# Products' columns 112 bytes past the weights: x, sources, memory and weight buffers at new places

## The chip, the cores and the metric

One Trainium2 chip, one core. The metric is device time in microseconds of one execution of the program; a run's time is taken on the chip, and a profiled execution gives the trace.

## What is computed

Two layers of a streaming-encoder trunk on 256 tokens of width 1024, in float32. Each layer is half a SwiGLU FFN, a mixer, cross-attention to a memory of 256 tokens, and half an FFN again:

```python
for layer in range(DEPTH):                       # 2
    x = x + 0.5 * swiglu(rms_norm(x, ffn_norm[layer, 0]), ...)
    h = rms_norm(x, mix_norm[layer])
    if layer % 2 == 0:
        x = x + diff_stickbreak_mixer(h, ab_w_in[i], ab_w_out[i], ...)
    else:
        x = x + mla_mixer(h, mla_w_dq[i], ..., mla_w_o[i])
    x = x + memory_cross_attention(rms_norm(x, xm_norm[layer]), rms_norm(mem, xm_mem_norm[layer]), ...)
    x = x + 0.5 * swiglu(rms_norm(x, ffn_norm[layer, 1]), ...)

def swiglu(h, w_gate, w_up, w_down):             # 1024 -> 2816 -> 1024
    return (jax.nn.silu(h @ w_gate) * (h @ w_up)) @ w_down
```

All products with weights (gate, up, down, the projections of the mixers and of the cross-attention) read 190 MB of weights once.

## The kernel before

Each float32 operand of a weight product is split into a high and a low part in a 4-byte format that TensorE multiplies in one pass (F32R), and a product is the sum of three: high by high, high by low, low by high. In `mm3` (lines 290 to 292) these are three matmuls of 256 streamed columns. In `mm2` (lines 285 and 286), used for the down and output products, high and low of the source lie side by side and are streamed as one matmul of 512 columns over the high weights, and then the high part as one of 256 over the low weights. The first operand of a matmul is the side that is loaded into the array (128 columns), the second is the side that streams. The load for the next matmul (LDWEIGHTS) is an instruction of its own beside the running matmul.

Who is loaded and who streams: in `fm` and `fm_g` (gate and up of the FFNs, the query products and some of the mixers) the weights are loaded and x streams, 48 matmuls for one weight tile of 128 x 2048. In `tm_g` (the other projections of the first mixer, and keys and values of the memory) x or the memory is loaded and the weights stream, 48 matmuls also. In the two MLA products `kv_product` and `q_product` the latent sources are loaded. In `mm2` the weights are loaded and the sources stream.

Weights: `issue` starts the DMA of a weight tile (`wr`), ScalarE copies it into the high part (`wh`, line 247) and VectorE (for some pieces GpSimd) subtracts for the low part (`wl`, line 249). Three buffers of each (`HL = 3`) go round in turn. Each buffer is 64 columns wider than the weights, and `W_AT` says at which column they start in the buffer whose turn it is: 0, 16 or 32 (0, 64 or 128 bytes).

x: the two parts xh and xl stand in one tile each, 64 columns wider than the eight blocks of 256. `begin_phase` takes the next place of `X_AT` and `finish_dt` writes the scaled and split blocks of x there (lines 485, 486). The nine phases are: the input of the first FFN, then what the first mixer, the first cross-attention, the second and the third FFN, the second mixer, the second cross-attention and the last FFN read, and the output. The places before are 4, 4, 4, 12, 20, 20, 20, 28 and 0.

Sources: `Pair` takes a slot of 1024 columns (two blocks, high and low of each) from the arena. Each slot is a tile of 1032 columns, of which columns 4 to 1028 are used. The FFNs have 11 such slots, the mixers 6; the arena is opened anew for each of five stages. Memory: eight tiles of 512 columns, high and low of four pairs of blocks, written by `mem_gain` during an FFN.

The order of TensorE's instructions is the order in which the program is written (in the mixers a planner with given costs writes it); the other engines are ordered by the tile framework. Places in memory play no part in either.

Of the kernel before, what the change touches and what calls it, by code (L numbers as in the profile page):

```python
# [12 lines left out]
F32R = mybir.dt.float32r  # L13
# [6 lines left out]
P = 128  # L20
# [45 lines left out]
MLA_ORDER = (('k', 0), ('kv', 0), ('kv', 1), ('q', 0), ('q', 1), ('k', 1), ('q', 2), ('q', 3), ('v', 0))  # L66
HL = 3

W_AT = (0, 16, 32)
X_AT = (4, 4, 4, 12, 20, 20, 20, 28, 0)  # L70
SLOTS_MIX = (29, 12)

MEM_AT = (2, 4, 6, 8)
# [84 lines left out]
def trunk_kernel(ctx, tc, wflat, xT_d, xtok_d, memT_d, memtok_d, gains_d, rows_d, cst_d, out_d):  # L158
# [3 lines left out]
    wpool = ctx.enter_context(tc.tile_pool(name="w", bufs=1))  # L162
    cpool = ctx.enter_context(tc.tile_pool(name="c", bufs=1))
# [4 lines left out]
    def nm(s):  # L168
        uid[0] += 1
        return f"{s}_{uid[0]}"  # L170

    def T(tag, shape, bufs, dt=F32, pool=apool):
        return pool.tile(shape, dt, tag=tag, bufs=bufs, name=nm(tag))


    ar = {}

    @contextmanager
    def arena(n32, n32r):
        with tc.tile_pool(name=nm("ar"), bufs=1) as pool:  # L180
            ar["f"] = [pool.tile([P, 512], F32, name=nm("slotf")) for _ in range(n32)]
            ar["r"] = [pool.tile([P, 1032], F32R, name=nm("slotr"))[:, 4:1028] for _ in range(n32r // 2)]
            ar["own"] = {}
            yield
            assert not ar["own"]
# [26 lines left out]
    offs, o = [], 0  # L212
# [3 lines left out]
    loaded = {}  # L216
    issued = [0]

    turn = [0]

    def buffers(i):
        key, w = plan[i]
        small = w <= 256
        sfx, width = ("s", 256) if small else ("", 2048)
        raw = T("wr" + sfx, [P, width], 1 if small else RAW, F32, wpool)
        if small:
            return (raw, *(T(n + sfx, [P, width], 1, F32R, wpool) for n in ("wh", "wl")))
        o = W_AT[turn[0] % HL]
        turn[0] += 1
        lo = T("wl", [P, width + 64], HL, F32R, wpool)  # L230
        hi = T("wh", [P, width + 64], HL, F32R, wpool)
        return raw, hi[:, o:o + width], lo[:, o:o + width]

    def issue(i):
        raw, hi, lo = buffers(i)
        w = plan[i][1]
        name = plan[i][0][0] if isinstance(plan[i][0], tuple) else plan[i][0]
        step = SPLIT if name in ("gate", "up", "down") else SPLIT_MIX
        np_ = 0 if name in ("gate", "up", "down") else POOL_OF.get(name, 512)
        dstep = w if name in ("gate", "up", "down") else DSTEP  # L240
        src = wflat[offs[i]:offs[i] + P * w].rearrange("(p w) -> p w", p=P)
        for a in range(0, w, step):
            if a % dstep == 0:
                b = min(a + dstep, w)
                nc.sync.dma_start(raw[:, a:b], src[:, a:b])
            b = min(a + step, w)
            A.copy(hi[:, a:b], raw[:, a:b])  # L247
            e = G if a >= w - np_ else V
            e.tensor_tensor(out=lo[:, a:b], in0=raw[:, a:b], in1=hi[:, a:b].bitcast(F32), op=ALU.subtract)  # L249
        loaded[i] = (hi, lo)  # L250
# [4 lines left out]
    def issue_part(i, h, n):  # L255

        if h == 0:
            first[:] = buffers(i)
            loaded[i] = tuple(first[1:])
            issued[0] = i + 1  # L260
        raw, hi, lo = first
        w = plan[i][1]
        a0, a1 = h * (w // n), (h + 1) * (w // n)
        nc.sync.dma_start(raw[:, a0:a1], wflat[offs[i]:offs[i] + P * w].rearrange("(p w) -> p w", p=P)[:, a0:a1])
        return lambda: split_part(raw, hi, lo, a0, a1)
# [243 lines left out]
    parts = [cpool.tile([P, KT * S + 64], F32R, name="x" + h) for h in "hl"]  # L509
    x_at = list(X_AT)  # L510

# [277 lines left out]

    memstate = {}  # L790

    mem_hl = [cpool.tile([P, 512], F32R, name=f"mem{q}{h}") for q in range(4) for h in "hl"]
    memstate["rs"], msum = small[:, 16:18], small[:, 20:24]

    def mem_gain(l, q):
# [688 lines left out]
    with arena(*SLOTS_FFN):  # L1484
        begin_phase()
        for h in range(4):
            if h:
                nc.sync.dma_start(x[:, 2 * h:2 * h + 2, :], xT_d[:, 2 * h:2 * h + 2, :])
            split_w = issue_part(0, h, 4)
            if h == 0:  # L1490
                nc.sync.dma_start(gains[:, 0:NG], gains_d)
            for dt in (2 * h, 2 * h + 1):
                for made in finish_dt(dt, G_FFN):
                    pin(made)
            split_w()
        for h in range(2):
            issue_part(1, h, 2)()

        st.xg = st.nxt
        st.rs, st.var, st.rb = sl()[:, 0:2], sl()[:, 0:2], T("rb", [P, S], 1)  # L1500
        ss = sm()
        for q in range(4):
            xt = al()
            nc.sync.dma_start(xt, xtok_d[:, q // 2, (q % 2) * 512:(q % 2 + 1) * 512])
            A.activation(xt, xt, AF.Square, accum_out=ss[:, q:q + 1])
            rel(xt)
        nc.sync.dma_start(cst, cst_d[:, 0:512])
        V.tensor_reduce(out=st.var, in_=ss[:, 0:4].rearrange("p (a b) -> p a b", b=2), axis=AX.X, op=ALU.add)
        V.tensor_scalar(out=st.var, in0=st.var, scalar1=1.0 / D, scalar2=EPS, op0=ALU.mult, op1=ALU.add)
        rsqrt(st.var, 2, st.rs)  # L1510
        st.todo = [spread]
        ffn(0, 0, G_MIX, True, 0)
    with arena(*SLOTS_MIX):
        mixer_ab(G_XM)
        cross(0, G_FFN + 8)
    with arena(*SLOTS_FFN):
        ffn(0, 1, G_FFN + 16, True)
        ffn(1, 0, G_MIX + 8, False, 1)
# [80 lines left out]
```

## Time and profile before

| | us |
|---|---|
| median of 3 runs | 1115.44 (1114.12 to 1117.67) |
| profiled execution | 1115.93 |
| its span | 1114.2 |
| TensorE busy (matmuls) | 1091.3, 98% of the span |
| VectorE busy | 792.6, 71% |
| ScalarE busy | 654.6, 59% |
| mean granted clock of TensorE | 0.997 |

The span is from the first to the last instruction of the program in the trace; the profiled execution's own time has some 1.7 us around it. A busy share of TensorE says that it had a matmul in flight, not how fast matmuls follow one another; that is read from their starts.

### The profile page before, as it was taken

Reading aid. Unit: us, or ns where it says so; the run is one execution under the profiler, and the core shown is the slowest. Engines: PE = TensorE matmul, PEld = TensorE weight load, DVE = VectorE, ACT = ScalarE, POOL = GpSimd, SP = SyncE. Lnnn points to the kernel's source line nnn. Section 1 sums busy time; section 2 is a strip of 40 time slices with the busy share of each in tenths; the row PEclk is TensorE's granted clock in tenths of the full one; section 3 lists DMA queues with packets and bytes.
Section 4 is the critical chain, followed back from the end, with each engine's and each line's share of the span. In section 5 each row is a group of like instructions: output and inputs, shape, how many; then the busy total and the mean of one; then the engine's idle time right before and its main releaser. Section 6 shows DMA issues by size and latency. Waiting matters only on the chain.

```text
span 1114.2 us, 21671 instructions
## 1 busy us (share of the span) xinstructions
PE 1091.3 (98%) x8144; PEld 1032.4 (93%) x8144; DVE 792.6 (71%) x1930; ACT 654.6 (59%) x1775; POOL 198.7 (18%) x210
## 2 busy tenths in 40 slices
PE   8999999999899999999999999999989999999998
PEld 8999988998889899998899999889868899999987
DVE  6887766667866887775777776655688768877653
ACT  6676554667656665554555555555866556555542
POOL 2100001366334200000100000114871422000000
PEclk9999999999999999999999999999999999999999
DMA  8766556535335265555556554554341443655561
GB/s 294 242 238 211 180 181 204 190 97 170 114 114 189 88 215 190 189 180 183 186 184 222 179 210 173 190 189 161 105 131 60 152 149 119 225 189 190 182 222 51
DMA packets 50794, 193.25 MB, mean 173 GB/s; under 512 B 5760, under 2 KB 7552, under 8 KB 35584
## 3 DMA queue, kind: packets, MB, share of 16 engines
q1 hardware_dynamic: 50688, 191.86, 50.1%
q8 instruction: 64, 1.05, 0.4%
q14 instruction: 42, 0.34, 0.1%
HBM read 190.79 MB, written 1.05 MB: 172 GB/s over the span
## 4 chain that ended last, share of the span: by engine, by line
PE 85%; DVE 6%; ACT 3%; POOL 2%; issue 2%; DMA 2%; SPq 0%; DVEq 0%; POOLq 0%; ACTq 0%
PE mm L290 18%; PE mm L291 18%; PE mm L292 18%; PE mm L285 18%; PE mm L286 9%; DVE wl L249 2%; DMA wr<-wflat 2%; ACT slotf L766 1%; POOL sm L471 1%; PE t L779 1%; PE t L479 1%; PE s L1430 0%; PE s L903 0%; PE o L1463 0%; POOL sl L471 0%
## 5 line engine op out<-in xcount | busy, mean ns | idle before, releaser
L247 ACT CAST wh<-wr 128x256 fp32r<-128x256 f32 (+1 forms) x1216 | 440.8, 434 | 316.6 <-PE mm L291 155.4
L249 DVE TENSOR_TENSOR wl<-wr,wh 128x256 fp32r<-128x256 f32 (+1 forms) x1171 | 481.8, 465 | 125.1 <-ACT wh L247 117.7
L290 PE MATMUL mm<-xh,wh 128*128 128x256 f32 x1584 | 445.2, 281 | 2.7 <-ACT wh L269 1.7
L292 PE MATMUL mm<-xh,wl 128*128 128x256 f32 x1584 | 443.1, 280 | 0.1
L291 PE MATMUL mm<-xl,wh 128*128 128x256 f32 x1584 | 443.1, 280 | 0.0
L285 PE MATMUL mm<-slotr,wh 128*128 128x512 f32 x896 | 315.9, 396 | 1.1 <-DVE slotr L486 1.1
L290 PEld LDWEIGHTS mm<-xh,wh 128*128 128x128 f32 x1584 | 297.9, 188 | 4.1 <-ACT wh L269 2.1
L292 PEld LDWEIGHTS mm<-xh,wl 128*128 128x128 f32 x1584 | 298.2, 188 | 0.6 <-DVE wl L270 0.4
L291 PEld LDWEIGHTS mm<-xl,wh 128*128 128x128 f32 x1584 | 297.9, 188 | 0.3 <-DVE xl L486 0.2
L286 PE MATMUL mm<-slotr,wl 128*128 128x256 f32 x896 | 251.5, 281 | 0.0
L285 PEld LDWEIGHTS mm<-slotr,wh 128*128 128x128 f32 x896 | 168.5, 188 | 40.9 <-DVE slotr L486 1.4
L286 PEld LDWEIGHTS mm<-slotr,wl 128*128 128x128 f32 x896 | 168.8, 188 | 0.1
L543 POOL TENSOR_TENSOR acc<-acc,sq 128x256 f32<-128x256 f32 x49 | 43.3, 884 | 470.7 <-ACT sq L535 466.8
L249 POOL TENSOR_TENSOR wl<-wr,wh 128x512 fp32r<-128x512 f32 x45 | 66.8, 1485 | 108.6 <-ACT wh L247 108.6
L726 DVE TENSOR_TENSOR slotf<-mm,rb 128x512 f32<-128x512 f32 x44 | 30.3, 688 | 55.9 <-PE mm L292 55.9
L522 DVE SCALAR_TENSOR_TENSOR x<-mm,x 128x256 f32<-128x256 f32 x128 | 52.1, 416 | 21.3 <-PE mm L286 20.8
L485 ACT ACTIVATE xh<-x,gains 128x256 fp32r<-128x256 f32 x64 | 32.1, 507 | 33.2 <-DVE x L522 29.4
L718 DVE TENSOR_TENSOR slotf<-mm,rb 128x512 f32<-128x512 f32 x44 | 30.3, 688 | 26.0 <-PE mm L292 26.0
L766 ACT ACTIVATE slotf<-s,sm,sl 128x256 f32<-128x256 f32 (+1 forms) x64 | 32.8, 523 | 23.6 <-DVE sm L760 18.0
L486 DVE SCALAR_TENSOR_TENSOR xl<-x,gains,xh 128x256 fp32r<-128x256 f32 x64 | 39.1, 617 | 5.3 <-ACT xh L485 5.2
L491 DVE TENSOR_TENSOR slotr<-slotf,slotr 128x512 fp32r<-128x512 f32 (+1 forms) x52 | 35.5, 686 | 3.0 <-ACT slotr L490 2.6
L290 PE MATMUL mm<-wh,xh 128*128 128x256 f32 x128 | 37.2, 291 | 0.0
(218 smaller groups left out, 1086.1 us busy)
## 6 DMA issues: line engine op xcount, KB each, us to landing
wr<-wflat SPq DMA_DIRECT2D x118, 1024.0 KB, 4.8
wr<-wflat SPq DMA_DIRECT2D x180, 256.0 KB, 3.9
wr<-wflat SPq DMA_DIRECT2D x16, 768.0 KB, 4.4
slotf<-memT SPq DMA_DIRECT2D x8, 256.0 KB, 3.2
x<-xT SPq DMA_DIRECT2D x4, 256.0 KB, 4.7
wr<-wflat SPq DMA_DIRECT2D x2, 512.0 KB, 8.1
slotf<-xtok SPq DMA_DIRECT2D x4, 256.0 KB, 8.0
slotf<-memtok SPq DMA_DIRECT2D x4, 256.0 KB, 3.5
```

The source lines that it names most:

```text
L247: A.copy(hi[:, a:b], raw[:, a:b])
L249: e.tensor_tensor(out=lo[:, a:b], in0=raw[:, a:b], in1=hi[:, a:b].bitcast(F32), op=ALU.subtract)
L285: PE.matmul(bank[:, 0:512], w[0], src[2], start=first, stop=False)
L286: PE.matmul(bank[:, S:512], w[1], src[0], start=False, stop=last)
L290: PE.matmul(out, a[0], b[0], start=first, stop=False, **kw)
L291: PE.matmul(out, a[0], b[1], start=False, stop=False, **kw)
L292: PE.matmul(out, a[1], b[0], start=False, stop=last, **kw)
L486: V.scalar_tensor_tensor(out=lo, in0=src, scalar=g, in1=hi.bitcast(F32), op0=ALU.mult, op1=ALU.subtract))
L491: V.tensor_tensor(out=lo, in0=src, in1=hi.bitcast(F32), op=ALU.subtract)
L522: V.scalar_tensor_tensor(out=xd, in0=ps[:, h * S:(h + 1) * S], scalar=factor, in1=xd, op0=ALU.mult, op1=ALU.add)
L543: G.tensor_tensor(out=st.acc, in0=st.acc, in1=sq, op=ALU.add)
L766: A.activation(p[:, i * w:(i + 1) * w], sps[:, i * w:(i + 1) * w], AF.Exp, bias=nb[:, i:i + 1], scale=r, accum_out=sums[:, i:i + 1])
```

## The change

The weight buffers lose their extra columns and their turning places: all six start at the same residue by 256 bytes. The parts of x are written at column 28 (112 bytes) in all phases but the second, where it is column 36 (144 bytes). The source slots of an arena become pieces of one tile, 4096 bytes apart, from column 28 on. The eight memory tiles become pieces of one tile, from column 36 on. The sizes of the tiles change by some hundred bytes; no instruction is named in the diff.

```diff
-W_AT = (0, 16, 32)
-X_AT = (4, 4, 4, 12, 20, 20, 20, 28, 0)
+
+COLUMNS, ROWS = 28, 36
+
+X_AT = (COLUMNS, ROWS) + 7 * (COLUMNS,)
...
-            ar["r"] = [pool.tile([P, 1032], F32R, name=nm("slotr"))[:, 4:1028] for _ in range(n32r // 2)]
+            rows = pool.tile([P, n32r // 2 * 1024 + 64], F32R, name=nm("slotr"))
+            ar["r"] = [rows[:, COLUMNS + i * 1024:COLUMNS + (i + 1) * 1024] for i in range(n32r // 2)]
...
-    turn = [0]
-
...
-        o = W_AT[turn[0] % HL]
-        turn[0] += 1
-        lo = T("wl", [P, width + 64], HL, F32R, wpool)
-        hi = T("wh", [P, width + 64], HL, F32R, wpool)
-        return raw, hi[:, o:o + width], lo[:, o:o + width]
+        return (raw, *(T(n, [P, width], HL, F32R, wpool) for n in ("wh", "wl")))
...
-    mem_hl = [cpool.tile([P, 512], F32R, name=f"mem{q}{h}") for q in range(4) for h in "hl"]
+    mem_rows = cpool.tile([P, 8 * 512 + 64], F32R, name="mem")
+    mem_hl = [mem_rows[:, ROWS + i * 512:ROWS + (i + 1) * 512] for i in range(8)]
```

## Rows read from the trace of the kernel before

**Rows 1.** Busy time of TensorE: us, share of the span, instructions (the page).

```profile
PE 1091.3 (98%) x8144; PEld 1032.4 (93%) x8144; DVE 792.6 (71%) x1930; ACT 654.6 (59%) x1775; POOL 198.7 (18%) x210
```

**Rows 2.** Longest of TensorE's waits: waiter, releaser, us in total, times, longest.

```profile
PE t L779 <- DVE slotf L838: 3.3, 2, 2.0
```

**Rows 3.** Busy times in a gate/up stretch (second FFN), granted clock, DMA share.

```profile
core 0: us, PE busy (x) PEld busy (x) DVE busy (x) ACT busy (x) POOL busy (x), PEclk, DMA share, GB/s
...
390.00:500.00 110.00, 110.00 (x932) 110.00 (x932) 81.25 (x203) 64.03 (x185) 0.00 (x0) 1.00 0.56 195
```

**Rows 4.** Timeline, last FFN: starts of products at 112, 48, 240, 112.

```profile
start us, us, engine line op out<-in xcount [idle before <-releaser]
1026.26 0.28 PE L290 MATMUL mm<-xh,wh 128*128 128x256 f32 x1
...
1031.71 0.28 PE L290 MATMUL mm<-xh,wh 128*128 128x256 f32 x1
...
1037.39 0.28 PE L290 MATMUL mm<-xh,wh 128*128 128x256 f32 x1
...
1043.02 0.28 PE L290 MATMUL mm<-xh,wh 128*128 128x256 f32 x1
```

**Rows 5.** Timeline of the weight loads, beside the second row above.

```profile
1031.72 0.19 PEld L291 LDWEIGHTS mm<-xl,wh 128*128 128x128 f32 x1
```

**Rows 6.** Timeline, second FFN: three products (144 matmuls) from first to last.

```profile
452.22 0.28 PE L290 MATMUL mm<-xh,wh 128*128 128x256 f32 x1
...
469.25 0.28 PE L290 MATMUL mm<-xh,wh 128*128 128x256 f32 x1
```

**Rows 7.** Timeline, first FFN: three products (144 matmuls) likewise.

```profile
66.83 0.28 PE L290 MATMUL mm<-xh,wh 128*128 128x256 f32 x1
...
83.63 0.28 PE L290 MATMUL mm<-xh,wh 128*128 128x256 f32 x1
```

**Rows 8.** Timeline, third FFN: three products (144 matmuls) likewise.

```profile
639.38 0.28 PE L290 MATMUL mm<-xh,wh 128*128 128x256 f32 x1
...
656.26 0.28 PE L290 MATMUL mm<-xh,wh 128*128 128x256 f32 x1
```

**Rows 9.** Groups of instructions (the page): the matmuls of 512 columns.

```profile
L285 PE MATMUL mm<-slotr,wh 128*128 128x512 f32 x896 | 315.9, 396 | 1.1 <-DVE slotr L486 1.1
```

**Rows 10.** Timeline, last down stage: first and last pair, 175 pairs apart.

```profile
1048.47 0.39 PE L285 MATMUL mm<-slotr,wh 128*128 128x512 f32 x1
...
1109.74 0.40 PE L285 MATMUL mm<-slotr,wh 128*128 128x512 f32 x1
```

**Rows 11.** Timeline, last down stage: a slot at 112, and the next.

```profile
1071.58 0.39 PE L285 MATMUL mm<-slotr,wh 128*128 128x512 f32 x1
1071.80 0.28 PE L286 MATMUL mm<-slotr,wl 128*128 128x256 f32 x1
...
1072.27 0.39 PE L285 MATMUL mm<-slotr,wh 128*128 128x512 f32 x1
```

**Rows 12.** Timeline, first mixer, x loaded, distance 112: 31 matmuls apart.

```profile
220.63 0.28 PE L290 MATMUL mm<-wh,xh 128*128 128x256 f32 x1
...
224.35 0.28 PE L291 MATMUL mm<-wl,xh 128*128 128x256 f32 x1
```

**Rows 13.** Timeline, first mixer, x loaded, distance 48: 23 matmuls apart.

```profile
235.06 0.28 PE L291 MATMUL mm<-wl,xh 128*128 128x256 f32 x1
...
237.75 0.28 PE L290 MATMUL mm<-wh,xh 128*128 128x256 f32 x1
```

**Rows 14.** Timeline, MLA stage, memory loaded, distance 0: 44 matmuls apart.

```profile
773.17 0.28 PE L290 MATMUL mm<-wh,mem0h 128*128 128x256 f32 x1
...
778.45 0.28 PE L292 MATMUL mm<-wh,mem3l 128*128 128x256 f32 x1
```

**Rows 15.** Timeline, MLA stage, product dq, distance 16: 24 matmuls apart.

```profile
761.12 0.28 PE L290 MATMUL mm<-xh,wh 128*128 128x256 f32 x1
...
763.84 0.28 PE L290 MATMUL mm<-xh,wh 128*128 128x256 f32 x1
```

**Rows 16.** Timeline of all engines, start of the MLA stage: a write, a read.

```profile
755.90 0.96 DVE L486 SCALAR_TENSOR_TENSOR xl<-x,gains,xh 128x256 fp32r<-128x256 f32 x1
...
756.43 0.28 PE L291 MATMUL mm<-xl,wh 128*128 128x256 f32 x1
```

## The prediction

> **What bounds the kernel now.** I read the page first, then the busy times by stretch, then the timeline of the matmuls, in which the start of one matmul against the start of the next is its pace. TensorE is busy for 98% of the span [rows 1], and the longest wait of any one kind on it adds up to 3.3 us [rows 2]. [...] So the sum of the paces of the matmuls is the time, and what is to be read is one pace against another. Durations in the rows (0.28 us) are no use for that, because matmuls overlap.
>
> Each gate or up product is 48 matmuls of 256 columns. In the last FFN four products follow one another [rows 4]: 1026.26 to 1031.71 is 5.45 us, or 113.5 ns a matmul; the next takes 5.68 us (118.3 ns), the next 5.63 us (117.3 ns). Same engine load, same shapes, same x. What differs is the place of the weight buffer: x lies at column 28 (112 bytes), the three buffers at columns 0, 16 and 32 (0, 64, 128 bytes), and in the built program both kinds of tile begin 128 bytes past a multiple of 256. The distance from the columns that a matmul streams to the weights loaded meanwhile for the next one is 112, 48 and 240 bytes (by 256). The weight load does run beside the matmul: it starts 0.01 us after it [rows 5]. The other FFNs give the other distances: 5.68 us on average with 48, 240 and 176 (17.03 us for three products [rows 6]); 5.60 us with 16, 208 and 144 (16.80 us [rows 7]); 5.63 us with 80, 16 and 208 (16.88 us [rows 8]). No other distance of these comes near 5.45 us, and all eight gate/up products at 112 run at 113.3 to 113.7 ns a matmul in the same view; one is shown.
>
> **The change part by part.** It removes the turning places of the weight buffers (all start at the same residue now), puts x at column 28 in every phase but the second (column 36, where x is mostly the loaded side), and source slots at column 28 and memory at column 36 of single tiles. No instruction is added, removed or moved. The sum is made against the profiled run, 1115.93 us (span 1114.2), which is 0.5 us above the median of the three runs, 1115.44.
>
> Gate/up. All four FFNs get distance 112, so each product should take 5.45 us. First FFN: its first three products wait for DMA, 19 are left, 19 x (5.60 - 5.45) = 2.9 us [rows 7]. Second: 22 x (5.677 - 5.45) = 5.0 us [rows 6]. Third: 22 x (5.627 - 5.45) = 3.9 us [rows 8]. Last: 7 x 0.23 + 7 x 0.18 = 2.9 us [rows 4]. Together 14.7 us, all on the path, since nothing but TensorE fills these stages. DVE would go from 81/110 to about 84% there, so it does not become the bound.
>
> Feature-major products of the mixers at column 28 (both cross queries, ckv and dq, seven in all): one runs at 113.3 ns already (24 matmuls in 2.72 us [rows 15]); six gain 0.15 to 0.23 us each, 1.1 us; bounds 0 (if other work ends last) and 1.4.
>
> Down and output products are pairs, 512 columns and then 256, 896 of them [rows 9]. Over the last down stage a pair takes 61.27 us / 175 = 350.1 ns [rows 10]. Their slots are 4128 bytes apart now, so the distance walks by 32 bytes from slot to slot. The two pairs of one slot at 112 take 0.69 us, 345 ns each [rows 11]; over the 82 undisturbed pairs at 112 I work out 347.2 from the same view. 896 x (350.1 - 347.2) = 2.6 us. Bounds: 0, and 11 us if pairs that are all at 112 settle at the shortest 512 (0.22 to 0.23 us [rows 11]) and the shortest 256 (113.5 ns), about 338 together. I take 347.2, which comes from the very distance.
>
> Products with weights streaming and x or memory loaded (eight and eight, 48 matmuls each) get 112 too, and here the rows speak against the change. The three x products that are at 112 now run at 120.0 ns (3.72 us for 31 [rows 12]), those at 48 at 117.0 (2.69 us for 23 [rows 13]); memory at distance 0 at 120.0 (5.28 us for 44 [rows 14]). If 120 holds for all, two x products lose 3 ns, three about 1.5 and five memory products about 2: 20 x 48 = 1.0 us lost. Bounds: 1.5 us lost; 3.8 us gained if they settle at 113.5 like gate/up. I take the loss, the row with the same side streaming.
>
> The ckv and cq sources become the loaded side at -112, that is 144: 144 matmuls by a few ns, within 0.5 us either way, counted 0. The qb and kb products get 144, which is among the distances of [rows 7]: 0.
>
> Single tiles. I cost them at nothing, since pieces of one tile are waited for separately now: from 755.90 DVE writes a piece of xl for 0.96 us, and at 756.43, meanwhile, a matmul reads another piece of that tile [rows 16]. The cover at a change of arena is that TensorE reads the last sources before the first matmul of the next stage; without it, four changes by one evacuation each would be some 4 us.
>
> Sum: 1115.9 - 14.7 - 1.1 - 2.6 + 1.0 = 1098.5; against the median some 1098 us.
>
> [...] The trace shows 113.5 and 118.3 ns in neighbouring products that differ in nothing but the place of the weights [rows 4]. [...]
>
> **The rivals.** First, the distance counts by 512, not by 256. In gate/up at 113.5 now, hi over hi and lo over lo are both 368 by 512, while the weight-streaming products at 120.0 are 112 by 512. After the change weight buffers are 8192 bytes apart and x hi and lo 33 x 256, so two of three gate/up matmuls would be at 112 and one at 368: (2 x 120.0 + 113.5)/3 = 117.8 against 117.1 now (4060 starts), 4080 x 0.7 = 2.9 us lost. Memory, all at 368, gains about 2.0, x loaded (two of three at 368) 1.0, pairs 2.6: 1113 us. For it: it explains 113.5 beside 120.0 at one distance. Against: 208 in the first FFN and 208 + 256 in the third run alike, and so do 240 and 240 + 256 in the second and last.
>
> Second, on the other side: the pace isn't set by the distance alone, and gate/up settles at the 120.0 that the same distance gives in [rows 12]. That there is more than one state for one place is shown by distance 16, which runs at 113.3 in [rows 15] and at 116.7 within [rows 8] with the same buffers. Price: 4080 x (120.0 - 117.1) = 11.8 us lost, less 2.6 and plus 1.0: 1126 us. It decides from two thirds of the gate/up matmuls at 120 on: the other gains carry a mean of 117.8, and (117.8 - 113.5)/(120.0 - 113.5) is 0.66. Against it: every gate/up product now at 112 settles at 113.5, whatever ran before it.
>
> Third, places do nothing and 113.5 belongs to something else in that third of the products: 1115.9. Against it stand all of [rows 4 to 8].
>
> **How the numbers follow.** Forecast 0.75, first rival 0.12, second 0.07, third 0.06. The predicted time is the forecast's, 1098. The range goes down to 1087 (the pairs' bound and the gain of the weight-streaming products nearly in full: 1115.9 - 14.7 - 1.4 - 9 - 3.8) and up to 1113, the first rival. What a measurement can tell from no change is about 0.3%, 3.3 us, so faster means under 1112.1: the forecast and a little of the first rival, 0.78; same 0.15; slower 0.07.
>
> **What would show it.** Right: four gate/up products in a row at 5.45 us in each FFN; pairs at 347 ns or less; x and memory products at 120.0. If gate/up shows two starts of three near 120, the first rival holds; all near 120, the second. The prediction is wrong by the pairs or by the weight-streaming products if these leave 347 and 120; and by the single tiles if TensorE's waits at the stage changes grow past the 3.3 us of [rows 2].

## The result, and the profile after

| | before | after |
|---|---|---|
| median | 1115.43 us (1114.12 to 1117.67) | 1103.96 us (1102.14 to 1105.31) |
| ratio of the medians | | 0.989 [0.987, 0.991] |
| profiled execution | 1115.93 | 1103.84 |
| its span | 1114.2 | 1102.1 |

The change takes 11.5 us off the median and 12.1 us off the profiled execution, where the sum had 17.4. The first thing to read is again the page of the kernel after, here the busy times, and then TensorE's waits (waiter, releaser, us in total, times, longest):

```profile
PE 1079.7 (98%) x8144; PEld 1019.4 (92%) x8144; DVE 793.3 (72%) x1930; ACT 654.9 (59%) x1775; POOL 196.1 (18%) x210
```

```profile
PE s L1428 <- DVE slotf L1415: 2.6, 1, 2.6
PE t L776 <- DVE slotf L836: 2.3, 2, 1.9
PE mm L287 <- DVE slotf L715: 2.0, 1, 2.0
```

The instructions are the same 8144 and TensorE is still busy for 98% [rows 1]: what changed is how fast they follow one another. The third wait is new, and it comes back below. In the gate/up stretch of the second FFN the busy times by window show 963 matmuls where 932 stood [rows 3]:

```profile
390.00:500.00 110.00, 110.00 (x963) 109.59 (x962) 84.39 (x209) 66.22 (x189) 0.00 (x0) 1.00 0.55 200
```

The timeline of the last FFN answers to [rows 4]. The rows are 48 matmuls apart:

```profile
1004.82 0.28 PE L288 MATMUL mm<-xl,wh 128*128 128x256 f32 x1
...
1010.26 0.28 PE L288 MATMUL mm<-xl,wh 128*128 128x256 f32 x1
...
1015.70 0.28 PE L288 MATMUL mm<-xl,wh 128*128 128x256 f32 x1
...
1021.14 0.28 PE L288 MATMUL mm<-xl,wh 128*128 128x256 f32 x1
```

Three times 5.44 us, 113.3 ns a matmul, one product like the next. Every gate/up product of the four FFNs looks so, but for the first ones of each stage, which hold a wait. The last down stage answers to [rows 10], first and last pair, 175 pairs apart:

```profile
1035.98 0.39 PE L282 MATMUL mm<-slotr,wh 128*128 128x512 f32 x1
...
1097.80 0.40 PE L282 MATMUL mm<-slotr,wh 128*128 128x512 f32 x1
```

61.82 us / 175 = 353.3 ns a pair, against 350.1 before: the pairs became slower, not faster. The products with x or the memory loaded answer to [rows 12] and [rows 14], in the timelines of the first mixer (57 matmuls apart) and of the MLA stage (47 apart):

```profile
231.84 0.28 PE L288 MATMUL mm<-wl,xh 128*128 128x256 f32 x1
...
238.67 0.28 PE L288 MATMUL mm<-wl,xh 128*128 128x256 f32 x1
...
762.73 0.29 PE L287 MATMUL mm<-wh,mem 128*128 128x256 f32 x1
...
768.38 0.28 PE L289 MATMUL mm<-wh,mem 128*128 128x256 f32 x1
```

6.83 us / 57 = 119.8 and 5.65 us / 47 = 120.2 ns.

To set the stages side by side I took the time from a stage's first weight product to the next stage's (the first FFN is cut at the matmul that starts at 28 us in the kernel before; what lies ahead of it is the first row). Profiled executions, us; the kernels of the last five columns come below:

| stage | before | after | slots back | high at 16 | pairs (0, 192) | entry 64 | entry 112 |
|---|---|---|---|---|---|---|---|
| start | 21.0 | 21.9 | 21.0 | 20.4 | 21.0 | 23.1 | 22.7 |
| gate/up 1 | 105.9 | 104.5 | 102.9 | 102.9 | 102.9 | 102.9 | 102.9 |
| down 1 | 61.6 | 62.2 | 61.8 | 61.0 | 61.6 | 60.4 | 60.3 |
| first mixer | 181.9 | 179.8 | 180.9 | 179.5 | 180.8 | 179.9 | 181.3 |
| gate/up 2 | 125.7 | 120.7 | 120.7 | 120.7 | 120.7 | 120.7 | 120.7 |
| down 2 | 61.9 | 62.2 | 61.8 | 61.0 | 61.6 | 60.4 | 60.3 |
| gate/up 3 | 124.8 | 120.7 | 120.7 | 120.7 | 120.7 | 120.7 | 120.7 |
| down 3 | 61.7 | 62.2 | 61.8 | 61.0 | 61.6 | 60.4 | 60.3 |
| MLA stage | 173.2 | 173.5 | 172.6 | 172.5 | 172.2 | 173.7 | 173.5 |
| gate/up 4 | 123.6 | 120.7 | 120.7 | 120.7 | 120.7 | 120.7 | 120.7 |
| down 4 | 61.5 | 62.1 | 61.7 | 60.9 | 61.5 | 60.3 | 60.1 |

The gate/up and down stages repeat to 0.1 us wherever the places are the same. The start, the first gate/up stage and the two mixers move by 1 to 3 us between kernels that do the same there (the last three kernels have the same mixers, and they differ by 1.4 and 1.5 us); that is the noise against which everything else is to be seen.

### The profile page after: what moved, and what is told of

It is laid out like the page before. It is cut to its first block, busy times and chain, and to the rows that moved or that the text cites. A ratio compares the mean times of both kernels' runs of the same rounds, so it can differ in the third digit from the quotient of the medians.

```text
span 1102.1 us, 21671 instructions
## 1 busy us (share of the span) xinstructions
PE 1079.7 (98%) x8144; PEld 1019.4 (92%) x8144; DVE 793.3 (72%) x1930; ACT 654.9 (59%) x1775; POOL 196.1 (18%) x210
## 4 chain that ended last, share of the span: by engine, by line
PE 87%; DVE 6%; ACT 3%; POOL 2%; issue 1%; DMA 1%; SPq 0%; DVEq 0%; ACTq 0%; POOLq 0%
PE mm L282 19%; PE mm L287 18%; PE mm L288 18%; PE mm L289 18%; PE mm L283 10%; DVE wl L246 2%; ACT slotf L763 1%; PE t L776 1%; POOL sm L468 1%; PE s L1428 1%; DMA wr<-wflat 1%; PE t L476 1%; PE s L901 0%; PE o L1461 0%; DMA gains<-gains 0%
## 5 line engine op out<-in xcount | busy, mean ns | idle before, releaser
L287 PE MATMUL mm<-xh,wh 128*128 128x256 f32 x1584 | 439.6, 278 | 4.1 <-DVE slotf L715 2.0
L289 PE MATMUL mm<-xh,wl 128*128 128x256 f32 x1584 | 437.6, 276 | 0.1
L288 PE MATMUL mm<-xl,wh 128*128 128x256 f32 x1584 | 437.3, 276 | 0.2 <-DVE xl L483 0.2
L287 PE MATMUL mm<-wh,mem 128*128 128x256 f32 x128 | 38.0, 297 | 0.0
```

Of the source, the lines that this page charges most:

```text
L287: PE.matmul(out, a[0], b[0], start=first, stop=False, **kw)
L288: PE.matmul(out, a[0], b[1], start=False, stop=False, **kw)
L289: PE.matmul(out, a[1], b[0], start=False, stop=last, **kw)
```

## The experiments

A distance below is from the columns that a matmul streams to the weights loaded next, by 256 bytes; a pair has two, (512-column matmul, 256-column matmul). In the records quoted here, theories are lettered anew for each run.

**Slots at their old places.** One edit of the changed kernel:

```diff
-            rows = pool.tile([P, n32r // 2 * 1024 + 64], F32R, name=nm("slotr"))
-            ar["r"] = [rows[:, COLUMNS + i * 1024:COLUMNS + (i + 1) * 1024] for i in range(n32r // 2)]
+            ar["r"] = [pool.tile([P, 1032], F32R, name=nm("slotr"))[:, 4:1028] for _ in range(n32r // 2)]
```

> The changed kernel with one part undone: the source slots are separate tiles of 1032 columns again, used from column 4 on (32 bytes further from slot to slot); x, memory and weights stay as changed. Theory A (the pairs of down and output products settle at 353.3 ns when all stand at 112, where the forecast took 347.2 from two pairs at a time): the pairs go back to about 350.1 ns, 896 x 3.2 ns = 2.9 us, so about 1101 us. Theory B (the place of the slots plays no part in the pace, the weight buffers' new places made the pairs slower): pairs stay near 353 and the time near 1104.

Measured: 1099.56 us, ratio 0.985 [0.983, 0.988]. The last down stage in its timeline, 175 pairs:

```profile
1031.97 0.40 PE L281 MATMUL mm<-slotr,wh 128*128 128x512 f32 x1
...
1093.40 0.40 PE L281 MATMUL mm<-slotr,wh 128*128 128x512 f32 x1
```

61.43 us, 351.0 a pair against 353.3, where theory A had 350.1: every down stage is 0.4 us shorter than after the change. So the change's slots, all at (112, 112), cost time by themselves, and the weights' new places leave the pairs no faster than before. The four down stages show 1.6 us less; the medians are 4.4 us apart (from different chips: the ratios 0.989 and 0.985 have intervals that touch), and in the two profiles 2.5 us of the difference stand in the start and the first gate/up stage, ahead of all slots (see the tables, below).

**x at its old columns.** One edit of the changed kernel:

```diff
-X_AT = (COLUMNS, ROWS) + 7 * (COLUMNS,)
+X_AT = (4, ROWS, 4, 12, 20, 20, 20, 28, 0)
```

> The changed kernel with x back at the columns of before (4, 12, 20 and 28 for the four FFNs, 4 and 20 ahead of them), weights, slots and memory as changed. Each FFN's gate and up products then stand at one distance throughout: 16, 48, 80 and 112. If the distance by 256 sets the pace (A): 5.45 us a product only in the last FFN; 5.60 in the first (or 5.45, if 16 settles at the quicker of the two states that were seen), 5.68 in the second, 5.68 to 5.75 in the third; in all about 10 us above the changed kernel. If an unbroken row of like products is what brings 113.5 ns (B): 5.45 us in all four, and the changed kernel's time.

Measured: 1118.35 us, a single run. Each gate/up stage now has one distance for all its products, and a pace of its own: 16 runs at 116.7 ns, 48 at 118.3, 80 at 118.4, 112 at 113.3. The second FFN (48) in the timeline, one product:

```profile
405.69 0.28 PE L289 MATMUL mm<-xh,wl 128*128 128x256 f32 x1
...
411.37 0.28 PE L289 MATMUL mm<-xh,wl 128*128 128x256 f32 x1
```

5.68 us, as 48 took before the change in the last FFN [rows 4], where it came from other columns (x at 28, weights at 16, here 12 and 0). The gate/up stages of the first three FFNs take 105.9, 125.8 and 125.9 us, so their gain is gone (the third is 1.1 us slower than before), while the last, still at 112, keeps its 120.7; everything else of the change is there. So here the pace goes with the distance, and in a row of equal products (118.3 ns at 48) as in a row of unequal ones (118.3 there too).

**Maps.** To see the pace at other distances I gave each product its own columns in the weight buffers (64 wider again), a different pair of distances to each of the 16 down products, and one to each product with x or the memory loaded:

```diff
+    def weights_at(key):
+        if key[0] == "down":
+            _, l, j, dp, _ = key
+            return GRID[(l * 2 + j) * 4 + dp]
...
+        oh, ol = weights_at(key)
+        hi = T("wh", [P, width + 64], HL, F32R, wpool)
+        lo = T("wl", [P, width + 64], HL, F32R, wpool)
+        return raw, hi[:, oh:oh + width], lo[:, ol:ol + width]
```

The first two maps differ in the slots' column (28, 20) and so in their distances; the third has slots at column 16, and qb and kb at 112.

> A map of distances, not meant to be quick: the weights of each quarter of a down stage lie at another pair of columns, high and low parts apart (0, 16, 32, 48 columns each, sixteen combinations), slots at column 28, so that the 512-column matmul and the 256-column one have distances 112, 48, 240 and 176 in every combination. The products with weights streaming get eight distances for x (112, 144, 176, 208, 240, 16, 48, 80) and eight for the memory (128, 160, 192, 224, 0, 32, 64, 96). Gate and up as changed, 113.4 ns. Theory A (settled pace by distance): the combination 112 and 112 gives 353 again although the weight buffers are a little wider here; some combinations settle below 347. Theory B (it is the equal places of the buffers by 512): 112 and 112 gives 347 or less. x at 112 stays at 119 to 120, x at 48 gives 117.

> The same map with slots at column 20: distances 80, 16, 208 and 144 for the two matmuls of a pair in every combination; x loaded at eight distances in steps of 16 between 120 and 232, memory likewise. By the means at these distances in the kernel before, pairs alike at 80 give about 352, at 16 350.6, at 208 354, at 144 347.7; if these were states passed through and not settled ones, as at 112, they come out elsewhere by up to 6 ns. Gate and up as changed, 113.4 ns.

> A third map: slots at column 16, high weights of down at another of four columns in each FFN and low ones in each quarter of it, so that both matmuls of a pair have distances 64, 0, 192 and 128 in every combination; x loaded at eight distances in steps of 32 (128 to 96 round), memory at 112, 144, 176, 208, 240, 16, 48, 80; qb and kb with weights at column 8, so that x streams at 112 there too. Nothing below 346.7 a pair is expected if that is a floor (the first two maps give it four times each and nothing less); qb and kb go from 117.5 to 113.5; memory at 48 gives 117, x at 192 what memory gave there (115.5).

Measured, a single run each: 1099.98, 1097.45 and 1101.11 us. In the first two maps I had cut the memory's tile to size, which moved the arena: the pairs' distances were made of 16, 80, 144 and 208, and of 48, 112, 176 and 240; the table has those that ran, from the addresses in the built programs, and not those of the two texts. ns a pair, 42 to 46 pairs of one down product each:

| distances | 340.0 to 340.5 | 346.6 to 347.0 | 348.9 to 352.2 | 353.0 to 360.0 |
|---|---|---|---|---|
| first map | | (144,208) (208,80) (144,144) (80,16) | (80,144) (208,16) (144,16) (80,80) (208,208) (80,208) (144,80) (208,144) | (16,144) (16,80) (16,208) (16,16) |
| second map | | (112,48) (48,176) (112,240) (48,240) | (176,112) (176,176) (240,112) (176,48) (48,48) | (240,176) (176,240) (112,176) (48,112) (112,112) (240,48) (240,240) |
| third map | (0,192) | (0,0) (128,0) (64,128) (192,0) (192,128) (128,64) | (128,192) (0,64) (64,0) (128,128) (0,128) | (64,64) (192,192) (64,192) (192,64) |

The slowest is (16,16) in the first map, 360.0 ns in every pair of its product, where the pairs at (16,16) before the change, between others, had a mean of 350.8. The fastest, (0,192), lies below the floor of 346.7 that the third text had.

Two products of the second map in its timeline, first (112, 112), then (112, 48), 43 pairs each:

```profile
705.43 0.40 PE L300 MATMUL mm<-slotr,wh 128*128 128x512 f32 x1
...
720.63 0.40 PE L300 MATMUL mm<-slotr,wh 128*128 128x512 f32 x1
...
1060.90 0.39 PE L300 MATMUL mm<-slotr,wh 128*128 128x512 f32 x1
...
1075.80 0.39 PE L300 MATMUL mm<-slotr,wh 128*128 128x512 f32 x1
```

15.20 us / 43 = 353.5 and 14.90 / 43 = 346.5. The change's place for the pairs is among the worst of its map, in a program whose weight buffers lie otherwise (8448 bytes apart, 353.5 ns, instead of 8192, 353.3): the theory that pairs were slow because weight buffers lay at equal places by 512 falls. The weight-streaming products gave, in ns, x loaded: 113.7 at 192, 116.8 to 116.9 at 48 and 160, 117.8 to 118.5 at 0, 32, 64, 80, 112, 208 and 240, 119.6 to 120.0 at 16, 96, 128, 144, 176 and 224. With the memory loaded, 115.5 at 192, 116.7 to 117.4 at 48, 64 and 160, up to 121.4 at 208. The second map put them on odd multiples of 8 bytes instead of multiples of 16, and all of them took 119 to 122. Gate/up stayed at 113.3 throughout.

**High weights at column 16.** One edit of the changed kernel: the pairs go to (112, 48).

```diff
-        return (raw, *(T(n, [P, width], HL, F32R, wpool) for n in ("wh", "wl")))
+        oh = 16 if key[0] in ("down", "ab_o", "xo0", "mla_o", "xo1") else 0
+        hi = T("wh", [P, width + 64], HL, F32R, wpool)
+        return raw, hi[:, oh:oh + width], T("wl", [P, width], HL, F32R, wpool)
```

> The changed kernel with one edit: the high weights of the down and output products start at column 16 of their buffers, so that the 512-column matmul keeps 112 to the low weights and the 256-column one has 48 to the next high ones. Theory A (each of the two distances counts, as in the map, where 112 and 48 gave 346.7 ns a pair): 896 x (353.3 - 346.7) = 5.9 us less than the changed kernel on the same chip, about 1098. Theory B (the map's short stretches of 44 pairs don't settle, a whole stage will): 353 and the changed kernel's time.

Measured: 1097.69 us (1094.65 to 1100.85), ratio 0.985 [0.982, 0.987]; the changed kernel again, run beside it:

> The changed kernel itself, once more, to stand beside the next two on one chip. 1102 to 1105 us as before. If the 2.0 us wait at 29 us and the 16 matmuls at 213 ns behind it (about 3.4 us together) come and go from run to run, its times spread over 2 to 3 us and its granted clock over 0.992 to 0.998.

1102.17 us (1100.12 to 1104.59), ratio 0.988 [0.985, 0.990]. The last down stage of the kernel with the edit, 175 pairs:

```profile
1027.83 0.39 PE L284 MATMUL mm<-slotr,wh 128*128 128x512 f32 x1
...
1088.50 0.39 PE L284 MATMUL mm<-slotr,wh 128*128 128x512 f32 x1
```

60.67 us / 175 = 346.7 ns, as the map says, in some 870 pairs that follow one another. With the slots where the change put them and 64 bytes more on one operand, the pairs give the gain that I had forecast. (353.3 - 346.7) x 896 is 5.9 us; the four down stages show 4.6 us less, and the medians are 4.5 us apart. The changed kernel's own runs spread over 4.5 us here, where 2 to 3 were expected.

**The tables later.** After the change TensorE waits at the start of the first FFN, which it did not before:

```profile
28.99 0.35 PE L287 MATMUL mm<-xh,wh 128*128 128x256 f32 x1 [2.00 <-DVE slotf L715]
...
30.04 0.41 PE L289 MATMUL mm<-xh,wl 128*128 128x256 f32 x1
30.25 0.41 PE L287 MATMUL mm<-xh,wh 128*128 128x256 f32 x1
...
33.24 0.35 PE L289 MATMUL mm<-xh,wl 128*128 128x256 f32 x1
```

Behind the wait of 2.00 us matmuls start 0.21 us apart from 30.0 to 33.2, where before has 0.12, and over 29 to 34 us the windows give a granted clock of 0.66, where before has 1.00 (first row after, second before):

```profile
29.00:34.00 5.00, 5.00 (x30) 5.00 (x31) 4.98 (x14) 4.10 (x12) 0.00 (x0) 0.66 0.83 313
```

```profile
29.00:34.00 5.00, 5.00 (x45) 5.00 (x44) 4.07 (x12) 4.06 (x12) 1.26 (x5) 1.00 0.76 247
```

TensorE waited for DVE's first evacuation, and the timeline of DVE and POOL shows what both did ahead of it. After:

```profile
22.18 5.12 DVE L246 TENSOR_TENSOR wl<-wr,wh 128x256 fp32r<-128x256 f32 x11
23.25 0.47 POOL L352 TENSOR_TENSOR dqa<-cst,slotf 128x128 f32<-128x128 f32 x1 [3.98 <-DMA slotf<-rows]
```

Before:

```profile
21.75 4.44 DVE L249 TENSOR_TENSOR wl<-wr,wh 128x256 fp32r<-128x256 f32 x13
23.23 3.88 POOL L355 TENSOR_TENSOR dqa<-cst,slotf 128x128 f32<-128x128 f32 x1 [3.82 <-DMA slotf<-rows]
```

Before, POOL's first table product takes 3.88 us while DVE does 13 pieces in 4.44 us, 0.34 each; after, the same POOL instruction takes 0.47 us and DVE needs 5.12 us for 11 pieces, 0.47 each. So in these two profiles the one engine is quick where the other is slow; I read that as one of them holding the other up, and which one differs from profile to profile. Of the thirteen profiles with the tables at this place, that POOL instruction takes 0.46 to 0.71 us and TensorE's wait is 1.9 to 2.2 us in six: after the change, in its repetition, with x at its old columns, in the third map and in the last two kernels below. It takes 3.73 to 3.91 us and the wait is 0.3 us or less in seven: before, with the slots back, in the first two maps, with the high weights at 16, and in the two kernels with all pairs at (0, 192). What decided between the two outcomes the rows do not show. The one costs TensorE some 1.7 us more of waiting than the other. To see what the start costs I moved the tables behind the fourth product block of the first FFN:

```diff
-                    setup()
...
             hs += h.blocks
+            if l == j == 0 and f == 3:
+                setup()
```

> The changed kernel with the setup of the tables (its DMAs, the GpSimd and the small DVE work) moved from behind the third product of the first FFN to behind its fourth pair of gate and up. If the wait at 29 us comes from GpSimd and DVE getting into each other's way there, it falls from 2.0 to 0.3 us or less, the clock stays at its upper level, and the kernel takes 1 to 3.4 us less than the changed one and spreads less. If the wait is DMA's (the first weights come late), nothing changes.

Measured: 1101.98 us (1100.12 to 1103.53), ratio 0.987, against 1102.17 for the changed kernel beside it. In its profile the wait is gone (none is listed from 24 to 34 us), matmuls start 0.11 us apart up to 29 us, and start and first gate/up stage together take 123.1 us instead of 126.4, and that profiled execution (1100.12) is 3.7 us shorter than after's; but the median is not. As the changed kernel's own runs reach from 1100.1 to 1105.3, some of them may not have had the wait, and the wait would then explain part of the spread and little of the median. That is argued, not shown: timed runs without a profile show no wait.

**All the best places at once, and the pairs alone at (0, 192).** Slots from column 16; weights of the down and output products at columns 32 (high) and 16 (low). The first of the two kernels also puts the weights of the products with x or the memory loaded at 192, and qb and kb at 112:

```diff
+        if key[0] in ("down", "ab_o", "xo0", "mla_o", "xo1"):
+            return 32, 16
+        if key[0] in ("ka", "qa", "vb", "va", "memk0", "memv0", "memk1", "memv1"):
+            return 20, 20
+        if key[0] in ("qb", "kb"):
+            return 8, 8
+        return 0, 0
```

> The changed kernel with each kind of product at the distance (by 256 bytes, streamed columns to the weights loaded next) that was shortest in the maps: gate/up stays at 112 (113.4 ns a matmul); slots start at column 16, and the weights of down and output products at columns 32 (high) and 16 (low), so that the 512-column matmul stands at 0 and the 256-column one at 192; x loaded and memory loaded, keys and queries of the first mixer (qb, kb): weights at columns 20 and 8, so that they stand at 192 and at 112. Theory A (the distance alone sets each pace, everywhere alike): pairs 340.4 ns instead of 353.2 (896 x 12.8 ns = 11.5 us), x loaded 113.7 instead of 119.3 (384 x 5.6 = 2.2 us), memory 115.5 instead of 119.6 (378 x 4.1 = 1.5 us), qb and kb some 4 ns less (190 x 4 = 0.8 us): 1103.3 - 16.0, some 1087 us. Theory B (340.4 and 113.7 belonged to the one product in which they were seen, and other products at the same distances settle at other levels, pairs at 346.7, x at 118): 1103.3 - 5.8 - 0.5 - 1.5 - 0.8, some 1094.5 us.

> The changed kernel with the pairs alone at 0 and 192 bytes: slots start at column 16, weights of down and output products at columns 32 (high) and 16 (low); nothing else moves. Theory A (the distance alone sets the pace of a pair): 340.4 ns a pair in all five stages, 896 x (353.2 - 340.4) = 11.5 us less than the changed kernel, some 1092 us. Theory B (340.4 was a state of the one product where it was seen): pairs at 346.7 like the best of the other distances, 5.8 us less, some 1097.5 us.

Measured: 1100.99 us (1097.22 to 1101.53), ratio 0.984 [0.983, 0.986], and 1098.63 us (1097.51 to 1099.25), ratio 0.983 [0.982, 0.985]; the kernel before, run beside them, took 1117.3 us, 1.9 more than its first median. The last down stage of the second, 175 pairs, and below it the product of the third map that had given 340.4, 43 pairs:

```profile
1031.01 0.39 PE L290 MATMUL mm<-slotr,wh 128*128 128x512 f32 x1
...
1092.26 0.40 PE L290 MATMUL mm<-slotr,wh 128*128 128x512 f32 x1
```

```profile
694.47 0.40 PE L299 MATMUL mm<-slotr,wh 128*128 128x512 f32 x1
...
709.11 0.39 PE L299 MATMUL mm<-slotr,wh 128*128 128x512 f32 x1
```

61.25 us / 175 = 350.0 against 14.64 / 43 = 340.5, at the same two distances and the same columns. Neither theory holds: the place does not fix the level, and 346.7 isn't what is left either. Even in one execution both occur: in the second kernel the output product of the first mixer's cross-attention (51 pairs from 315.4 on) runs at 340.0, all down products at 350.0. For the weight-streaming products the map did hold. With x loaded, 57 matmuls, and with the memory, 47, in the first kernel's timeline:

```profile
229.51 0.28 PE L300 MATMUL mm<-wl,xh 128*128 128x256 f32 x1
...
236.00 0.28 PE L300 MATMUL mm<-wl,xh 128*128 128x256 f32 x1
...
760.62 0.28 PE L299 MATMUL mm<-wh,mem 128*128 128x256 f32 x1
...
765.97 0.28 PE L301 MATMUL mm<-wh,mem 128*128 128x256 f32 x1
```

6.49 / 57 = 113.9 and 5.35 / 47 = 113.8 ns; over all of them 113.7 and 114.8, and qb and kb near 114. That makes 2.2 + 1.8 + 0.9 us of product time, but against the kernel with the pairs alone the first mixer became only 0.9 us shorter, and the MLA stage 1.5 us longer: there the second of the waits listed above, for DVE's attention work, is 3.0 us instead of 1.4. The median shows no gain; it is 2.4 us higher, and in the profiles 2.5 us of that lie in the start and the first gate/up stage, where this kernel's first weights came later (a wait of 2.6 us for ScalarE's copies, 1.1 in the other). In these two profiles TensorE's faster products in the mixers turned into longer waits for other engines; with one profile each, and mixers that move by as much without a cause in the program, that is not shown.

**What runs ahead of a pair.** In the third map the product at 340.4 came behind one at (64, 192), 353.2 ns. So, with all else as in the kernel of pairs at (0, 192), I moved the first of the four products in each down stage, once to (64, 192) and once to (112, 48):

```diff
+        if key[0] in ("down", "ab_o", "xo0", "mla_o", "xo1"):
+            return 32, 0 if key[0] == "down" and key[3] == 0 else 16
...
+        if key[0] == "down" and key[3] == 0:
+            return 4, 52
```

> As the kernel with all pairs at 0 and 192 bytes, with one edit: in each of the four down stages the low weights of the first product of four start at column 0 instead of 16, so that its pairs stand at 64 and 192. In the kernel with places mapped for slots at 64 such a product (353.2 ns a pair) came before the one product whose pairs settled at 340.4 at 0 and 192, while in the kernel with all pairs at 0 and 192 they settle at 350.0 in the down stages. Theory A (one place has two levels, and which one a run of pairs falls into depends on what ran before it; once in, it stays): products two to four of each down stage at 340.4, 4 x 131 x 9.6 ns = 5.0 us less and 4 x 44 x 3.2 = 0.6 us more, some 4.5 us below the kernel with all pairs at 0 and 192: ratio to before 0.979. Theory B (the level belongs to something else than the product before it): 350.0 in products two to four, ratio 0.984 as there.

> As the kernel with all pairs at 0 and 192 bytes, with one edit: in each of the four down stages the first product of four stands at 112 and 48 (low weights from column 52, high from column 4), where pairs ran at 346.7 ns everywhere. Theory A (what ran before decides between 340.4 and 350.0): the products behind it may fall into either level, alike in all four stages; with 340.4 the ratio to before is some 0.979, with 350.0 some 0.983. Theory B (the level belongs to something else than the product before it): 350.0 in all four stages, ratio 0.983.

Measured: 1097.79 us (1095.81 to 1099.6), ratio 0.984 [0.982, 0.986], and 1097.51 us (1094.52 to 1099.66), ratio 0.9835 [0.981, 0.986]. The last down stage in the timelines, first kernel: the first pair of all, then the first and last of the three products at (0, 192), 131 pairs apart:

```profile
1030.31 0.39 PE L290 MATMUL mm<-slotr,wh 128*128 128x512 f32 x1
...
1045.85 0.40 PE L290 MATMUL mm<-slotr,wh 128*128 128x512 f32 x1
...
1090.41 0.39 PE L290 MATMUL mm<-slotr,wh 128*128 128x512 f32 x1
```

44.56 us / 131 = 340.2, and 44 pairs of (64, 192) before in 15.54 us, 353.2. The second kernel: the product at (112, 48), 42 pairs, then 130 pairs:

```profile
1030.49 0.39 PE L292 MATMUL mm<-slotr,wh 128*128 128x512 f32 x1
...
1045.17 0.40 PE L292 MATMUL mm<-slotr,wh 128*128 128x512 f32 x1
1045.87 0.39 PE L292 MATMUL mm<-slotr,wh 128*128 128x512 f32 x1
...
1090.07 0.39 PE L292 MATMUL mm<-slotr,wh 128*128 128x512 f32 x1
```

44.20 / 130 = 340.0, and (112, 48) at 14.68 / 42 = 349.5, where the kernel with the high weights at 16 held 346.7 at these distances. All four down stages of both kernels do the same. So theory A of both texts holds in the down stages: with nothing but the first product moved, the three behind it go from 350.0 to 340.0 and stay there for 130 pairs. That what runs ahead decides the level everywhere is not shown, and the output products speak against it. Those of the first cross-attention have the same instructions and the same addresses in the kernel with all pairs at (0, 192) and in these two, back to the end of the down stage before, and start behind the same wait of 1.13 us. Yet 48 of their pairs, from first to last, take 15.98 us in that kernel and 16.45 us in the one with (64, 192) ahead:

```profile
316.49 0.39 PE L290 MATMUL mm<-slotr,wh 128*128 128x512 f32 x1
...
332.47 0.39 PE L290 MATMUL mm<-slotr,wh 128*128 128x512 f32 x1
```

```profile
316.31 0.39 PE L290 MATMUL mm<-slotr,wh 128*128 128x512 f32 x1
...
332.76 0.40 PE L290 MATMUL mm<-slotr,wh 128*128 128x512 f32 x1
```

That is 340.0 and 350.0 ns over 47 steps. It is 350.0 in the kernel with (112, 48) ahead and 353.3 in the kernel with all the best places. So one place holds at least three levels (340.0, 350.0, 353.3), and the long runs of pairs here kept the one that they fell into (340.2 ns over 131 pairs, 350.0 over 175); what makes the choice, beside the product ahead, stays open.

The four down stages are 4.6 and 5.3 us shorter than with all pairs at (0, 192). The ratio of 0.979 is missed, though. In the profiles 2.2 and 1.7 us are lost again at the start (the same wait, of 2.2 and 1.9 us, for DVE) and 1.5 and 1.2 in the MLA stage. The start lies ahead of all pairs, so this loss can't come from them. In the MLA stage the output products run at 353.3 instead of 350.0 ns in the larger of their two runs, which is 0.2 us; the rest stays open.

## Why the prediction was right, and where its sum was off

The time, 1104, lies in the range, the direction and the main mechanism hold, and the sum was 5.9 us too low. Step by step:

**Gate/up, 14.7 us forecast: 15.1 measured.** This was the mechanism of the forecast, and it came out as argued: every product at the pace that a third of the last FFN's products had. The paces went from 116.7, 118.2, 117.4 and 116.2 ns in the four FFNs to 113.3 to 113.5, worth 3.0, 5.0, 4.1 and 2.9 us, term by term what was written. It is visible whole in stages 2 to 4 (5.0, 4.1, 2.9); in the first only 1.4 us arrive, since the slow stretch behind the start's wait takes 1.6 back. TensorE is busy for all 110.00 us of the stretch in the second stage, before [rows 3] and after. One figure beside it was wrong: DVE's share of such a stage was put at 84% and measures 77% (84.39 us of 110, where 81.25 stood [rows 3]).

**Feature-major products of the mixers, 1.1 forecast: 0.9 measured.**

**Pairs, 2.6 gained forecast: 2.5 lost. This is the step that failed,** a miss of 5.1 us and nearly the whole error. The forecast was right all the same because gate/up is six times as large. I took 347.2 ns from the pairs that stood at 112 before the change. Those were two pairs of a slot, between pairs at other distances [rows 11]; what I read was a passing from one place to the next, not a settled pace. Settled, in a row of 44 pairs or more, (112, 112) runs at 353.3. I also bounded the cost at 0 from above, though nothing excluded a loss. The other bound, 338 a pair "at the shortest", was nearly reached: 340.0 exists, but at (0, 192) and there only in some of the runs of pairs.

**Weight-streaming products, 1.0 lost forecast: 0.7 lost.** x loaded went from 118.4 to 119.3, the memory from 118.6 to 119.6. Here the rows with the same side streaming were the right ones [rows 12], as argued. They were runs of 23 to 44 matmuls and not two pairs; that this is why they carried is likely, but was not tested.

**Single tiles and sources of the MLA, 0 forecast: 0.** No wait of TensorE at a change of arena is longer than before, but for 0.2 us for `xl` near the start of the MLA stage, and the slots in separate tiles show the same waits, these 0.2 us too.

**The remainder.** -15.1 - 0.9 + 2.5 + 0.7 is -12.8. The first weight product starts 0.6 us later, the start costs 0.9 in its own stage and 1.6 in the next: -9.7, where the profiled executions say -12.1. The missing 2.4 us are nearly all in the two mixers: these became 1.8 us shorter together, though the terms make them 0.4 longer (-0.9 + 0.7, and 0.6 for their pairs). This is a remainder that no trace here explains; the mixers differ by almost as much between kernels that are alike there. It nearly cancels the 3.1 us lost ahead of the pairs, which is luck.

**The rivals.** By 512: falls, since after the change gate/up matmuls alternate between 112 and 368 by 512 and all run at 113.3. Gate/up at 120: falls with it. Places do nothing: falls with x at its old columns, where moving x alone takes back the gain of three gate/up stages. With nothing but places moved, the same loads beside the same matmuls gave 113.3 to 118.4 ns in gate/up, 113.7 to 122 with weights streaming and 340.0 to 360.0 in pairs.

The changed kernel is not the best of these: with the pairs at (112, 48) it takes 1097.69 us, 0.9845 of before; the three kernels with pairs at (0, 192) alone or behind another entry lie within 1 us of that, which these runs can't tell apart.

## What to carry to other kernels

When a kernel is bound by matmuls that each load new weights, compare the pace of equal products at different places in memory before anything else is tuned; here 64 bytes on one operand were worth 4.6 us over four down stages. Read a pace only from a long run of one kind at one place (here 42 pairs and more), because a few matmuls between others show the passage and can have the wrong sign (two pairs of a slot gave 347.2 ns here, against a mean of 350.1; settled they took 353.3). And don't take a level seen once for a property of the place: move it into another neighbourhood and look again, and compare a second kernel that is the same there.

## What was not expected of the hardware

- Many settled paces stand on a few levels: pairs at 340.0, 346.7, 350.0, 353.3 and 360.0 ns, single matmuls often at 113.3, 116.7 and 120.0, all of them steps of 3.3 ns or twice that apart. Some places lie between, as gate/up at 48 with 118.3, or pairs of the maps with 348.9 and 352.2.
- One place can hold more than one of them: (0, 192) 340.0, 350.0 and 353.3, (112, 48) 346.7 and 349.5 (with other columns for both operands), and before the change a distance of 16 at 113.3 [rows 15] or 116.7.
- Who streams matters: at 112 the product with weights loaded runs at 113.3 ns, with weights streaming at 119.3; at 192 the latter runs at 113.7.
- Around the MLA stage's wait for DVE (2.6 us, first of the waits above, and as long before the change) the granted clock falls to 0.83 over 20 us after the change, and to 0.91 before; the window of after, then of before:

```profile
800.00:820.00 20.00, 17.03 (x94) 15.83 (x94) 15.46 (x42) 12.20 (x31) 12.98 (x17) 0.83 0.49 159
```

```profile
810.00:830.00 20.00, 16.10 (x98) 14.97 (x98) 16.65 (x44) 12.31 (x31) 14.65 (x17) 0.91 0.51 159
```

That is 0.08 x 20, some 1.6 us more at full clock lost after the change, an estimate from the two granted clocks. The kernel with (112, 48) ahead shows 0.83 around this wait too, the one with the high weights at 16 shows 0.91; why it is lower in some kernels is open.
